# A two-block transformer kernel: two thirds of the modulation vectors move from matrix products to row sums on the vector engine, and neighbouring transposes are issued in common runs

## The chip, the cores and the metric

One core of a Trainium2 chip runs the whole program. Its engines work side by side, each in the order of its own instruction list: TensorE (PE, with its weight loads PEld), VectorE (DVE), ScalarE (ACT), GpSimd (POOL), and SyncE (SP), whose queue issues the DMAs. The metric is the device time in microseconds (us); less is better.

## What is computed

Two blocks, each of two layers, over 256 tokens of width 1024. The first block has three kinds of attention, a gate and a layer norm. In the second block 256 context tokens join, and every layer begins with a modulation that depends only on two vectors, `c` and `c_ctx`:

```python
shift_x, scale_x, gate_x = jnp.split(jax.nn.silu(c) @ w_mod + b_mod, 3, axis=-1)
shift_c, scale_c, gate_c = jnp.split(jax.nn.silu(c_ctx) @ w_mod + b_mod, 3, axis=-1)
hx = rms_norm(xs, norm_g) * (1 + scale_x[:, None]) + shift_x[:, None]
hc = rms_norm(cs, norm_g) * (1 + scale_c) + shift_c
px = split_cols(hx @ w_in + b_in)
pc = split_cols(hc @ w_in + b_in)
# px, pc feed a convolution branch, a gated linear attention and an attention
xs = xs + gate_x[:, None] * merge(px, ya_x, yb_x, yc_x)
if need_ctx:                       # layer 0 only
    cs = cs + gate_c * merge(pc, ya_c, yb_c, yc_c)
```

`merge` is `(sigmoid(p13)*ya + sigmoid(p14)*yb + sigmoid(p15)*yc) @ w_out`. `w_mod` is 1024 x 3072 in each layer, so the modulation of both layers reads 24 MB of weights, and each weight takes part in just two products.

## The kernel before, in words

**Large products.** A large product is done as three passes of a reduced-precision format (`mm3`, lines 184 to 186): high times high, high times low, low times high. Each weight unit of 512 KB is loaded by SP into one of RAW = 4 buffers (`wr_...`), cast by ACT into `wh_...` (line 154, WB = 5 buffers) and subtracted by DVE into `wl_...` (line 155, 5 buffers). `WStream` holds one table of all units in the order of use. `get(key)` calls `ahead`, which issues loads up to `ad` table entries and splits up to `asp` entries beyond the one in use: 3 and 2 at first, 6 and 3 from the first block's output product on.

**The modulation.** Each layer has three vectors (s = 0 shift, 1 scale, 2 gate), and each of them is eight units of 512 KB: 48 units in all. `mod_stream` (lines 762 to 788) takes a unit as loaded, without a split, and multiplies it by a narrow stationary operand with `c` and `c_ctx` (line 770, four products of 256 columns, which the trace shows as eight instructions). After eight units ACT copies the sums (line 775), four small products turn them (line 778, tile `modt`), and DVE adds the bias (line 782). The table `FILL` says ahead of which weight unit how many modulation units are worked: all 24 of layer 0 in the second layer of block one, the 24 of layer 1 in block two, 16 in its layer 0 and 8 in its layer 1. `get` of that unit issues them. One PSUM buffer of the five tagged `gm` holds the running sums.

**Block two, layer 0** (`block2`), in its program order: keys (`AKV`, tokens in pairs of 128-token blocks) and queries (`AQ`, `BQ`), convolution inputs (`Va`, `Vb`), attention interleaved with `GK`, `GQ`, `GV` and `ag`; then the merges: branch `m3`/`oa`, gates `gg`, branch `m2`/`og`, `conv_finish`, gates `cg`, branch `m1`/`oc`, and the residual products `o` and `p`. A branch takes two gate units and one output unit in turn, so between `m3_1` and `oc3` there are 43 units. The convolution is 31 taps for each of four blocks, one DVE instruction each (line 1012); 10 are issued with each attention step, 24 with the `gg` gates and 32 among the merges of `m2`; `conv_finish` (from line 1330) needs them all. Layer 1 has the same parts in another order.

**Transposes.** A transpose is a PE instruction that copies a 128-wide tile through PSUM. `post_k` (line 925 on) makes two for each token block, `lrt` (line 938) right after the product and `akt` (line 952) after a norm and a rotation on DVE. In the attention, `weigh` ends with two (`ot`, line 1091) and `scores` with one (`mt`, line 1053).

**Order.** Within each engine the order is fixed when the program is built, by a planner that takes among ready instructions the one that comes first in the program. On the chip each engine then runs its list in that order, and an instruction that has to wait holds all behind it.

Of the kernel before, what the change touches and what calls it, by code (L numbers as in the profile page):

```python
# [33 lines left out]
WLX = 0  # L34
# [5 lines left out]
MORDER = (1, 0, 2)  # L40

FILL = '1B2 2 1E2 3 1D2 3 1F0 2 1G0 2 1H2 1 0Va0 2 0Va1 2 0Va2 2 0GV0 1 0ag0 2 0ag2 2 1GV0 3 1ag0 2 1ag2 2 1A0 1 0BQ2 2 1F2 2 1GK0 1 1B0 1 1A3 5 1C2 1 0ag1 1 1H0 1 0GK0 2'
# [68 lines left out]
class WStream:  # L111
# [46 lines left out]
    def whole(self, key):  # L158

        i = self.idx[key]  # L160
        self.ahead(i)
# [12 lines left out]
    def get(self, key):  # L174
# [4 lines left out]
        self.ahead(i)  # L179
        return self.spl[i]  # L180
# [49 lines left out]
def block1(g, l, xTh, xTl, xtok, W, last, pre_out=lambda: None, hold=None, each=None):  # L230
# [268 lines left out]
    def fox_gates():  # L499
# [24 lines left out]
        nc.tensor.matmul(ps[:, 128:256], lf[:, 0, :], g.ones, start=False, stop=True)  # L524
# [208 lines left out]
def units_mod():  # L733
    return [(f'mod{s}{k}', k, 1, [(D * s, D)]) for s in MORDER for k in range(8)]

# [26 lines left out]
def mod_stream(g, l, W):  # L762

    nc, sp, pp = g.nc, g.sp, g.pp
    for s in MORDER:
# [18 lines left out]
        if s == 1:  # L784

            nc.vector.scalar_tensor_tensor(g.modA[l], g.mod[l][:, ks, :], 1.0,
                                           g.ng[l][:, :, None].to_broadcast([128, 8, 2]), op0=OP.add, op1=OP.mult)
# [3 lines left out]
def norm_prep(g, l, seqs, hT, a, n):  # L791
# [6 lines left out]
    for j, (sT, w) in enumerate(seqs):  # L798
        pr = g.t2([128, 2, 256], f'{nm}pr{j}')
        for i in range(8 // nk):  # L800
# [36 lines left out]
def block2(g, l, hT, res_of, W, out=None, then=lambda x: None):  # L837
# [23 lines left out]
    def tm(key, nch, tbs, n, post, seq=False):  # L861
# [12 lines left out]
        for j in range(h):  # L874
            for tb in tbs:
                part(tb, [j])
        for tb in tbs:
            part(tb, range(h, nch))
            post(ps[tb][:, :n], tb)
# [28 lines left out]
    def rope2(x, nh, tb, which, nm):  # L908
# [10 lines left out]
        nc.vector.tensor_add(x, x, t)  # L919

    def gain(x, nh, which):
        x3 = x.rearrange("p (h d) -> p h d", d=64)
        nc.vector.tensor_mul(x3, x3, g.qkg[l][:, which, None, :].to_broadcast([128, nh, 64]))
# [4 lines left out]
    def post_k(ps, tb):  # L928
# [8 lines left out]
        pt = pp.tile([96, 128], F32, name=f'lrt{l}{tb}', tag='at', bufs=g.AT)  # L937
        nc.tensor.transpose(pt, kl[:, 128:224], idf)
        lr = lrT[:, 128 * tb:128 * tb + 128]
        nc.scalar.copy(lr[0:96], pt)  # L940
        nc.vector.tensor_sub(lr[32:64], pt[32:64], lr[32:64].bitcast(F32))
# [5 lines left out]
        if tb < 2:  # L947
            gain(kb, 2, 1)
        else:
            rope2(kb, 2, tb - 2, 1, f'k{tb}')  # L950
        pt = pp.tile([128, 128], F32, name=f'akt{l}{tb}', tag='at', bufs=g.AT)
        nc.tensor.transpose(pt, kb, idf)
        ts = slice(128 * tb, 128 * tb + 128)
# [4 lines left out]
        nc.vector.tensor_sub(k12[64:128, 0, 1, ts], pt[64:128], k12[64:128, 0, 1, ts].bitcast(F32))  # L958

# [62 lines left out]
    def scores(tb, kv):  # L1022
# [28 lines left out]
        nc.vector.scalar_tensor_tensor(ms[:, 1], mx, -1.0, ms[:, 0].bitcast(F32), op0=OP.mult, op1=OP.subtract)  # L1051
# [4 lines left out]
        yield  # L1056

    def weigh(tb, kv, q1, q2):
# [30 lines left out]
        pt = pp.tile([128, 2, 128], F32, name=nm + 'ot', tag='at', bufs=g.AT)  # L1089
        for i in range(2):  # L1090
            nc.tensor.transpose(pt[:, i, :], o[:, 128 * i:128 * i + 128], idf)
        c = 128 * tb - T0
        nc.scalar.activation(aoT[:, 2 * kv:2 * kv + 2, c:c + 128], pt, AF.Copy, scale=0.5)
        yield

    prev = iter(())
    for tb, kv in [(tb, kv) for tb in TB for kv in range(2)]:
        nxt = scores(tb, kv)
        qs = next(nxt)
        for st in range(4):  # L1100
            next(prev, None)
            next(nxt, None)
        prev = weigh(tb, kv, *qs)
    for _ in prev:
        pass

# [724 lines left out]
```

## Time and profile before

| what | us |
|---|---|
| median of 3 runs | 1193.03 |
| lowest and highest of them | 1192.88, 1195.18 |
| the profiled execution's own time | 1192.62 |
| its span, first to last instruction | 1190.8 |
| PE, DVE, ACT busy | 1168.5, 921.1, 569.5 |

A busy time is the time in which an engine has at least one instruction under way. PE's matmuls overlap, so the cost of one is read from start to start, not from its duration. A stretch is a piece of the span, counted in us from its start.

### The profile page before, as it was taken

The page shows a single profiled execution, that of the slowest core. Times are in us where ns is not written, and L with a number is a line of the kernel's source. Part 1 is how long each engine was busy: PE and PEld are TensorE (multiplying, and loading weights), DVE is VectorE, ACT ScalarE, POOL GpSimd, SP SyncE. Part 2 cuts the span into 40 slices and gives each one's busy share as a digit, 9 for nine tenths or more (in the row PEclk, how much of TensorE's full clock was granted, in tenths as well). Part 3 has the DMA queues.
Part 4 walks back from the last instruction along what each step waited for, and adds up shares of the span by engine and source line. Part 5 has one row for each costly group of instructions (what it writes and reads, how often), then busy time and mean ns, then how long its engine had stood idle before and what let it go on. Part 6 is the DMA issues. An engine that isn't in the chain of part 4 may idle for free.

```text
span 1190.8 us, 20632 instructions
## 1 busy us (share of the span) xinstructions
PE 1168.5 (98%) x8024; PEld 975.7 (82%) x8024; DVE 921.1 (77%) x2051; ACT 569.5 (48%) x1024; POOL 11.2 (1%) x42
## 2 busy tenths in 40 slices
PE   8999999999999999999999999999999999999998
PEld 6788777677887777767887888888999778999998
DVE  6996766967799859989545986755799897896984
ACT  5556634456555433247444422433455534855552
POOL 0000000000000000000000000000000000000000
PEclk9999999999999999999999999999999999999999
DMA  7634566465555642024221232325545333554552
GB/s 263 224 125 127 186 207 225 155 229 195 177 194 181 230 137 89 19 73 145 68 84 59 89 100 78 106 89 177 178 142 186 96 107 123 179 162 127 174 176 72
DMA packets 47538, 171.33 MB, mean 144 GB/s; under 512 B 5260, under 2 KB 5900, under 8 KB 46672
## 3 DMA queue, kind: packets, MB, share of 16 engines
q1 hardware_dynamic: 47440, 170.01, 43.7%
q8 instruction: 63, 1.03, 0.3%
q14 instruction: 35, 0.29, 0.1%
HBM read 167.89 MB, written 2.10 MB: 143 GB/s over the span
## 4 chain that ended last, share of the span: by engine, by line
PE 76%; DVE 11%; DMA 6%; ACT 5%; issue 2%; SPq 0%; ACTq 0%; DVEq 0%
PE f0m L186 3%; PE f0m L185 3%; PE f0m L184 3%; PE f1m L186 2%; PE f1m L184 2%; PE f1m L185 2%; PE po L185 1%; PE po L186 1%; PE po L184 1%; PE mod L770 1%; PE go L186 1%; PE go L185 1%; PE go L184 1%; PE yog L186 1%; PE yoc L186 1%
## 5 line engine op out<-in xcount | busy, mean ns | idle before, releaser
L1012 DVE SCALAR_TENSOR_TENSOR ucv<-up,par,ucv 128x512 f32<-128x512 f32 (+1 forms) x240 | 147.3, 614 | 2.8
L184 PE MATMUL f0m<-hTh,wh_0m 128*128 128x512 f32 x192 | 75.1, 391 | 0.0
L185 PE MATMUL f0m<-hTl,wh_0m 128*128 128x512 f32 x192 | 75.1, 391 | 0.0
L186 PE MATMUL f0m<-hTh,wl_0m 128*128 128x512 f32 x192 | 74.8, 390 | 0.0
L184 PE MATMUL f1m<-hTh,wh_1m 128*128 128x256 f32 x192 | 54.9, 286 | 0.1
L186 PE MATMUL f1m<-hTh,wl_1m 128*128 128x256 f32 x192 | 54.8, 286 | 0.0
L185 PE MATMUL f1m<-hTl,wh_1m 128*128 128x256 f32 x192 | 54.5, 284 | 0.0
L154 ACT CAST wh_0m<-wr_0m 128x1024 fp32r<-128x1024 f32 x24 | 25.1, 1047 | 55.9 <-PE f0m L185 14.5
L155 DVE TENSOR_TENSOR wl_0m<-wr_0m,wh_0m 128x1024 fp32r<-128x1024 f32 x24 | 29.3, 1222 | 18.2 <-ACT wh_0m L154 18.1
L184 PEld LDWEIGHTS f0m<-hTh,wh_0m 128*128 128x128 f32 x192 | 36.1, 188 | 7.4
L185 PEld LDWEIGHTS f0m<-hTl,wh_0m 128*128 128x128 f32 x192 | 36.1, 188 | 7.3
L186 PEld LDWEIGHTS f0m<-hTh,wl_0m 128*128 128x128 f32 x192 | 36.1, 188 | 7.3
L184 PEld LDWEIGHTS f1m<-hTh,wh_1m 128*128 128x128 f32 x192 | 36.8, 191 | 0.5 <-ACT wh_1m L154 0.3
L186 PEld LDWEIGHTS f1m<-hTh,wl_1m 128*128 128x128 f32 x192 | 36.7, 191 | 0.2 <-DVE wl_1m L155 0.2
L185 PEld LDWEIGHTS f1m<-hTl,wh_1m 128*128 128x128 f32 x192 | 36.8, 191 | 0.1
L154 ACT CAST wh_1m<-wr_1m 128x1024 fp32r<-128x1024 f32 x24 | 24.9, 1049 | 24.4 <-PE f1m L185 7.6
L155 DVE TENSOR_TENSOR wl_1m<-wr_1m,wh_1m 128x1024 fp32r<-128x1024 f32 x24 | 29.3, 1221 | 8.6 <-ACT wh_1m L154 8.4
L155 DVE TENSOR_TENSOR wl_0o<-wr_0o,wh_0o 128x1024 fp32r<-128x1024 f32 x8 | 9.8, 1224 | 13.2 <-ACT wh_0o L154 13.2
L1413 DVE SCALAR_TENSOR_TENSOR xT<-po,mod,xT 128x256 f32<-128x256 f32 x16 | 7.7, 483 | 14.3 <-PE po L186 14.3
L185 PE MATMUL po<-mgl,wh_0o 128*128 128x256 f32 x64 | 18.2, 285 | 0.0
L186 PE MATMUL pp<-mgh,wl_0p 128*128 128x256 f32 x64 | 18.2, 284 | 0.0
L185 PE MATMUL pp<-mgl,wh_0p 128*128 128x256 f32 x64 | 18.2, 284 | 0.0
(1857 smaller groups left out, 3960.6 us busy)
## 6 DMA issues: line engine op xcount, KB each, us to landing
wr_0mod<-in_wm_dram SPq DMA_DIRECT2D x24, 512.0 KB, 4.5
wr_1mod<-in_wm_dram SPq DMA_DIRECT2D x24, 512.0 KB, 3.7
wr_0m<-in_w_dram SPq DMA_DIRECT2D x24, 512.0 KB, 3.5
wr_1m<-in_w_dram SPq DMA_DIRECT2D x24, 512.0 KB, 3.5
wr_0O<-in_w1o_dram SPq DMA_DIRECT2D x8, 512.0 KB, 3.6
wr_1O<-in_w1o_dram SPq DMA_DIRECT2D x8, 512.0 KB, 3.6
wr_0o<-in_wo_dram SPq DMA_DIRECT2D x8, 512.0 KB, 3.6
wr_0p<-in_wo_dram SPq DMA_DIRECT2D x8, 512.0 KB, 3.7
```

Of the source, the lines that this page charges most:

```text
L154: g.nc.scalar.copy(wh, r)
L155: g.nc.vector.tensor_sub(wl, r, wh.bitcast(F32))
L184: nc.tensor.matmul(out, lh, rh, start=start, stop=False)
L185: nc.tensor.matmul(out, lh, rl, start=False, stop=False)
L186: nc.tensor.matmul(out, ll, rh, start=False, stop=stop)
L770: nc.tensor.matmul(ps[32 * q:32 * q + 32], g.cz[:, k // 2, 2 * (k % 2):2 * (k % 2) + 32], w[:, 0, 256 * q:256 * q + 256], start=k == 0, st ...
L1012: yield nc.vector.scalar_tensor_tensor(o, src, dw[:, i, j:j + 1], o, op0=OP.mult, op1=OP.add)
L1413: nc.vector.scalar_tensor_tensor(r[:, f, :], ps[:, :256], g.mod[l][:, 16 + f, w:w + 1], r[:, f, :], op0=OP.mult, op1=OP.add)
```

## The change

Modulation: only the 16 units of layer 0's scale and shift stay products (`MODP`), in the second layer of block one, at the places where they were. The other 32 units (layer 0's gate, all of layer 1) are laid out with the output index on the partitions (`pack_mod`), 256 outputs by 512 inputs in a unit. `mod_dots` multiplies each with the vector `c` or `c_ctx`, spread over all partitions, and sums the rows: four DVE instructions of 128x512 with a running sum to a unit. The vector is loaded and its silu made twice, once for each half. `DFILL` spreads the 32 units evenly over the 43 units from layer 0's `m3_1` to `oc3`; they are issued by `get` of that unit and stand in the load table one entry later (`LATE`).

Further: modulation entries no longer count in the look-ahead (`behind`); `wl` has four buffers instead of five (`WLX`); the all-ones matrix shrinks to a column, and the rotation table is loaded when needed, once for each layer, instead of lying in the constants.

Transposes: `post_k` returns its last DVE instruction and a `flip`, and both blocks' flips are issued together after the second; the first waits for the second block's DVE work. In the attention the `ot` transposes of one step wait for the `mt` transpose's input of the next. In `norm_prep` and `conv_finish` the first PE instruction of a run waits for the last DVE input of that run.

```diff
-WLX = 0
+WLX = -1
-FILL = '1B2 2 1E2 3 1D2 3 1F0 2 1G0 2 1H2 1 0Va0 2 0Va1 2 0Va2 2 0GV0 1 0ag0 2 0ag2 2 1GV0 3 1ag0 2 1ag2 2 1A0 1 0BQ2 2 1F2 2 1GK0 1 1B0 1 1A3 5 1C2 1 0ag1 1 1H0 1 0GK0 2'
+FILL = '1A0 1 1A3 5 1B0 1 1B2 2 1E2 3 1C2 1 1D2 3'
+DFILL = ((32, '0m3_1', '0oc3'),)
+LATE = 1
+MODP = [(0, 1), (0, 0)]
+MODD = [(*m, c, h) for ms, hs in (([], (0, 1)), ([(0, 2), (1, 1), (1, 0), (1, 2)], (1, 0)))
+        for h in hs for m in ms for c in range(4)]
...
+    def behind(self, i, n):
+        while n and i < len(self.table) - 1:
+            i += 1
+            n -= self.table[i][0] not in self.f32
+        return i
     def ahead(self, i):
-        while self.nd < min(len(self.table), i + self.ad + 1):
+        while self.nd < min(len(self.table), self.behind(i, self.ad) + 1):
             self._dma()
-        while self.ns < min(len(self.table), i + self.asp + 1):
+        while self.ns < min(len(self.table), self.behind(i, self.asp) + 1):
...
         self.ahead(i)
+        for _ in range(self.dots.pop(key, 0)):
+            next(self.dotstream)
         return self.spl[i]
...
+def mod_dots(g, W):
+    nc, sp = g.nc, g.sp
+    junk = g.cp.tile([128, 512], BF, name='modj')
+    have, seen = None, set()
+    for l, s, c, h in MODD:
+        if h != have:
+            cb, have = sp.tile([128, 2, 512], F32, name=f'modc{l}{s}{h}', tag='modc', bufs=1), h
+            nc.sync.dma_start(cb, g.csrc[1024 * h:1024 * h + 1024][None, :].to_broadcast([128, 1024])
+                              .rearrange("p (w k) -> p w k", w=2))
+            for w in range(2):
+                t = g.t2([128, 512], f'modt{l}{s}{h}{w}')
+                nc.scalar.activation(t, cb[:, w], AF.Tanh, scale=0.5)
+                nc.vector.scalar_tensor_tensor(cb[:, w], t, 1.0, cb[:, w], op0=OP.add, op1=OP.mult)
+        x = W.whole(f'{l}mod{s}{c}{h}')
+        m = g.mod[l][:, 8 * s:8 * s + 8, :]
+        second = (l, s, h ^ 1) in seen
+        if c == 0:
+            half = sp.tile([128, 8, 2], F32, name=f'modh{l}{s}', tag='modh', bufs=2) if second else m
+        for b in range(2):
+            for w in range(2):
+                nc.vector.scalar_tensor_tensor(junk, x[:, b], 0.5, cb[:, w], op0=OP.mult, op1=OP.mult,
+                                               accum_out=half[:, 2 * c + b, w:w + 1])
+        if c == 3:
+            seen.add((l, s, h))
+            if second:
+                nc.vector.tensor_add(m, m, half)
+                nc.vector.tensor_add(m, m, g.bmod[l][:, 8 * s:8 * s + 8, None].to_broadcast([128, 8, 2]))
+                if s == 1:
+                    mod_gain(g, l)
+        yield
...
         for tb in tbs:
             part(tb, range(h, nch))
-            post(ps[tb][:, :n], tb)
+            late.append(post(ps[tb][:, :n], tb))
+        if isinstance(late[0], tuple):
+            for i, (_, flip) in enumerate(late):
+                first = flip()
+                if i == 0:
+                    g.wait(first, late[1][0])
...
         for st in range(4):
-            next(prev, None)
-            next(nxt, None)
+            flip = next(prev, None) or flip
+            got = next(nxt, None) or got
+        if flip is not None:
+            flip(got)
...
-CST = [('ident', 128), ('ones', 128), ('rope2', 256), ('gmask', 256), ('sel8', 8), ('hm', 4), ('zc', 2)]
+CST = [('ident', 128), ('ones', 1), ('gmask', 256), ('sel8', 8), ('hm', 4), ('zc', 2)]
...
+    rc = g.t2([128, 2, 2, 64], f'rope2c{l}')
+    nc.sync.dma_start(rc, g.rope2src.rearrange("p (a t d) -> p a t d", a=2, t=2))
```

## Rows read from the trace of the kernel before

**Rows 1.** Page, part 1: busy us (share of the span) and instructions of each engine.

```profile
PE 1168.5 (98%) x8024; PEld 975.7 (82%) x8024; DVE 921.1 (77%) x2051; ACT 569.5 (48%) x1024; POOL 11.2 (1%) x42
```

**Rows 2.** Busy times by stretch: length, each engine's busy us (instructions), clock, DMA share, GB/s.

```profile
240.00:300.00 60.00, 55.36 (x449) 43.28 (x451) 40.19 (x93) 37.23 (x104) 0.17 (x2) 1.00 0.59 200
340.00:400.00 60.00, 59.08 (x348) 47.23 (x347) 58.08 (x218) 35.17 (x65) 0.00 (x0) 1.00 0.56 190
440.00:560.00 120.00, 119.19 (x900) 90.71 (x899) 109.05 (x181) 52.95 (x86) 3.23 (x7) 1.00 0.24 77
560.00:655.00 95.00, 93.55 (x730) 76.66 (x728) 51.95 (x106) 42.39 (x87) 0.00 (x0) 1.00 0.24 73
655.00:737.00 82.00, 81.76 (x366) 67.74 (x367) 65.19 (x88) 27.45 (x37) 0.17 (x2) 1.00 0.31 97
737.00:773.00 36.00, 35.91 (x173) 29.47 (x172) 30.21 (x76) 14.04 (x19) 0.46 (x6) 1.00 0.30 88
773.00:827.00 54.00, 54.00 (x240) 44.73 (x239) 25.27 (x30) 18.77 (x24) 0.00 (x0) 1.00 0.40 134
900.00:1000.00 100.00, 99.05 (x807) 81.44 (x807) 91.69 (x239) 41.75 (x76) 1.15 (x3) 1.00 0.35 114
```

**Rows 3.** PE's modulation products alone, by stretch: length, busy us (instructions), clock, DMA.

```profile
248.00:345.00 97.00, 5.10 (x64) 1.00 0.57 193
345.00:420.00 75.00, 4.28 (x64) 1.00 0.58 200
420.00:560.00 140.00, 5.92 (x64) 1.00 0.28 91
560.00:900.00 340.00, 0.00 (x0) 1.00 0.34 107
900.00:1010.00 110.00, 4.89 (x64) 1.00 0.39 125
```

**Rows 4.** PE's `modt` products alone, by stretch, in the same columns.

```profile
200.00:345.00 145.00, 1.22 (x8) 1.00 0.56 191
345.00:560.00 215.00, 1.08 (x8) 1.00 0.39 129
560.00:1010.00 450.00, 0.62 (x4) 1.00 0.35 111
```

**Rows 5.** PE in order of time around one `lrt` transpose: start, us, instruction.

```profile
365.17 0.29 PE L184 MATMUL t0AKV<-wh_0AKV,hTh 128*128 128x288 f32 x1
365.30 0.30 PE L185 MATMUL t0AKV<-wl_0AKV,hTh 128*128 128x288 f32 x1
365.71 0.29 PE L938 MATMUL lrt<-cst,kb 128*96 128x128 f32 x1
365.75 0.38 PE L186 MATMUL t0AKV<-wh_0AKV,hTl 128*128 128x288 f32 x1
365.97 0.30 PE L184 MATMUL t0AKV<-wh_0AKV,hTh 128*128 128x288 f32 x1
```

**Rows 6.** PE in order of time around the two `ot` transposes of a step.

```profile
448.34 0.39 PE L186 MATMUL f0GK<-hTh,wl_0GK 128*128 128x512 f32 x1
448.57 0.40 PE L184 MATMUL f0GK<-hTh,wh_0GK 128*128 128x512 f32 x1
448.80 0.38 PE L1091 MATMUL at000ot<-cst,at000o 128*128 128x128 f32 x2
448.94 0.36 PE L1044 MATMUL at001s<-k,at001q 128*128 128x256 f32 x1
449.14 0.28 PE L1045 MATMUL at001s<-k,at001q 128*128 128x256 f32 x1
```

**Rows 7.** DVE instructions by line: count, ns least/median/most, first and last start, shape.

```profile
L669 DVE SCALAR_TENSOR_TENSOR mx<-xtok,go x4: 680/681/689, 150.4 to 162.8; 128x512 f32<-128x512 f32 x4
L669 DVE DVE_READ_ACCUMULATOR mx<-xtok,go x4: 81/84/84, 151.0 to 163.4; 128x1 f32 x4
L431 DVE SCALAR_TENSOR_TENSOR lscr<-par x4: 206/216/218, 79.5 to 238.5; 128x64 f32<-128x64 f32 x4
L1274 DVE SCALAR_TENSOR_TENSOR qgg<-gtgg,qgg x4: 681/688/690, 656.8 to 673.2; 128x512 f32<-128x512 f32 x4
L1274 DVE SCALAR_TENSOR_TENSOR qgc<-gtgg,qgc x4: 418/419/420, 1065.0 to 1073.6; 128x256 f32<-128x256 f32 x4
```

**Rows 8.** The end of the convolution chain on DVE, and its first user on PE.

```profile
767.31 1.35 DVE L220 SCALAR_TENSOR_TENSOR ycg<-gtcg,ycg 128x512 fp32r<-128x512 f32 x2
...
773.30 0.39 PE L184 MATMUL yoc<-ycg,wh_0oc 128*128 128x512 f32 x1
```

**Rows 9.** Waits of the load queue, whole span: engine, line, releaser: us, times, longest.

```profile
SPq L130 <- DVE wl_0m L155: 134.7, 22, 13.1
SPq L130 <- PE mod L770: 90.4, 25, 14.2
```

**Rows 10.** The 31-tap convolution on DVE within 548 to 800 us.

```profile
L1012 DVE SCALAR_TENSOR_TENSOR ucv<-up,par,ucv 128x512 f32<-128x512 f32 x47 | 35.2, 749 | 0.6
```

More of the change, by code (lines that the diff above doesn't have):

```diff
@@ L733, in units_mod, with pack_mod @@
 def units_mod():
-    return [(f'mod{s}{k}', k, 1, [(D * s, D)]) for s in MORDER for k in range(8)]
+    return [(f'mod{s}{k}', k, 1, [(D * s, D)]) for _, s in MODP for k in range(8)]
+def pack_mod(l, w):
+    wt = w.T.reshape(24, 128, 2, 512)
+    parts = [pack(w, units_mod())] if l == 0 else []
+    for ll, s, c, h in MODD:
+        if ll == l:
+            f = 8 * s + 2 * c
+            parts.append(wt[f:f + 2, :, h].transpose(1, 0, 2).reshape(-1))
+    return np.concatenate(parts)
 def _seq(n, k):
@@ L946, in post_k, with flip_k @@
         nc.vector.tensor_mul(k3, k3, ky[:, :, None].to_broadcast([128, 2, 64]))
[L947 to L950, printed above, removed]
+        done = gain(kb, 2, 1) if tb < 2 else rope2(kb, 2, tb - 2, 1, f'k{tb}')
+        return done, lambda: flip_k(kl, tb)
+    def flip_k(kl, tb):
+        kb = kl[:, 0:128]
+        pl = pp.tile([96, 128], F32, name=f'lrt{l}{tb}', tag='at', bufs=g.AT)
+        first = nc.tensor.transpose(pl, kl[:, 128:224], idf)
         pt = pp.tile([128, 128], F32, name=f'akt{l}{tb}', tag='at', bufs=g.AT)
         nc.tensor.transpose(pt, kb, idf)
+        lr = lrT[:, 128 * tb:128 * tb + 128]
+        nc.scalar.copy(lr[0:96], pl)
+        nc.vector.tensor_sub(lr[32:64], pl[32:64], lr[32:64].bitcast(F32))
         ts = slice(128 * tb, 128 * tb + 128)
@@ L1088, in weigh, with flip @@
         nc.vector.tensor_mul(o.rearrange("p (h d) -> p h d", d=64), po[:, :, 0:64], rc.to_broadcast([128, 4, 64]))
[L1089 to L1094, printed above, removed]
+        def flip(after):
+            pt = pp.tile([128, 2, 128], F32, name=nm + 'ot', tag='at', bufs=g.AT)
+            for i in range(2):
+                t = nc.tensor.transpose(pt[:, i, :], o[:, 128 * i:128 * i + 128], idf)
+                if i == 0 and after is not None:
+                    g.wait(t, after)
+            c = 128 * tb - T0
+            nc.scalar.activation(aoT[:, 2 * kv:2 * kv + 2, c:c + 128], pt, AF.Copy, scale=0.5)
+        yield flip
     prev = iter(())
@@ L1348, in conv_finish @@
             for tb in range(NT // 128):
-                nc.tensor.transpose(pt[:, 128 * tb:128 * tb + 128], ns[tb][:, 128 * f:128 * f + 128], idf)
+                t = nc.tensor.transpose(pt[:, 128 * tb:128 * tb + 128], ns[tb][:, 128 * f:128 * f + 128], idf)
+                if f == tb == 0:
+                    g.wait(t, normed)
             tz = t2(f'cvz{f}', NT)
@@ L1654, in setup2 @@
     g.rowsrc = {}
+    g.rope2src = ins['rope2']
     rp = ins['rowp']
@@ L1726, in program @@
     nc = g.nc
-    mods = sum((table(ins[f'wm_{l}'], f'{l}', units_mod()) for l in range(2)), [])
-    f32 = {e[0] for e in mods}
+    mods = table(ins['wm_0'], '0', units_mod())
+    dots, at = [], [len(mods) * 128 * 1024, 0]
+    for l, s, c, h in MODD:
+        dots.append((f'{l}mod{s}{c}{h}', ins[f'wm_{l}'], at[l], 2, 512))
+        at[l] += 128 * 1024
+    f32 = {e[0] for e in mods + dots}
     fs = FILL.split()
@@ L1746, in program @@
         seq += o
+    keys = [e[0] for e in seq]
+    use, at, m = {}, {}, 0
+    for n, a, b in DFILL:
+        a, b = keys.index(a), keys.index(b) + 1
+        for i in range(n):
+            k = a + i * (b - a) // n
+            at.setdefault(keys[k + LATE], []).append(dots[m])
+            use[keys[k]] = use.get(keys[k], 0) + 1
+            m += 1
+    assert m == len(dots)
     tab, m = [], 0
@@ L1749, in program @@
         n = fills.get(e[0], 0)
-        tab += mods[m:m + n] + [e]
+        tab += mods[m:m + n] + at.get(e[0], []) + [e]
         m += n
@@ L1755, in program @@
     W = WStream(g, tab, looks, f32, fills)
-    W.stream = itertools.chain(mod_stream(g, 0, W), mod_stream(g, 1, W))
+    W.stream, W.dots, W.dotstream = mod_mm(g, W), use, mod_dots(g, W)
     xsp = g.dram.tile([128, 2048], F32, name='xsp')
```

64 lines of the change are left out of this document (35 added, 29 removed).

## The prediction

> **What bounds the kernel now.** I read the page's first part, then the busy times by stretch, then PE's own order in time where the change cuts in. PE is busy 98% of the span, DVE 77%, ACT 48% [rows 1]. The stretches say the same nearly everywhere: PE has 119.2 of 120 us in the attention of block two's layer 0 and 81.8 of 82 among the merges of `m2` [rows 2]. So whatever is taken out of PE's list shortens the kernel, as long as the other engines keep up. The reader should see in the same rows that DVE is close behind in places: 58.1 of 60 us at 340 to 400, 109.1 of 120 at 440 to 560, 91.7 of 100 at 900 to 1000, but only 52.0 of 95 at 560 to 655 and 25.3 of 54 at 773 to 827. The clock column is 1.00 in all of them, so the clock plays no part. The question is an exchange: PE time saved at one price, DVE time paid at another, in a stretch where DVE may or may not have it to give.
>
> The sum is made against the profiled execution, 1192.6 us (span 1190.8 and 1.8 around it); the median of the runs is 0.4 above it, which I add at the end. About 0.2%, 2.4 us, is what a measurement of this kernel can tell from no change.
>
> **PE: 32 units of products leave.** Their busy time by stretch is 5.1 us (8 units) at 248 to 345, 4.3 and 5.9 us (8 each) at 345 to 420 and 420 to 560, and 4.9 us (8) at 900 to 1010 [rows 3]: 20.2 us, 0.63 to a unit. Four of the six `modt` groups leave too, about 0.6 us each: one of the two at 200 to 345, both at 345 to 560, one later, 2.3 us [rows 4]. Gross 22.5 us. What arrives differs by stretch.
> - 248 to 345: gross 5.7. PE is already idle 4.6 of 60 us here, and DVE and ACT have a third free [rows 2]. The queue of loads waits 90 us in the whole span for modulation products to give their buffers back [rows 9], so eight units less also bring weights earlier. Against that, products that filled the waits of the attention saved nothing. I take 4, between 0 and 7.
> - 345 to 420: gross 4.8. DVE is full for most of it, with 1.9 us idle in 60 [rows 2], so PE would mostly wait instead. I take 1.5, between 0 and 4.8.
> - 420 to 560: gross 6.4. DVE's 109 us still fit into 113.6. I take 5.5, between 2 and 6.4.
> - 900 to 1010: gross 5.5. DVE's 91.7 us of 100 fit into 95. I take 4.5, between 1 and 5.5.
>
> Together 15.5 us, between 3 and 23.7.
>
> **PE: transposes in common runs.** The `lrt` transpose starts 0.41 us after a product that is otherwise followed in 0.13, and the second product behind it starts 0.67 after the first where 0.26 would do: one transpose alone costs 0.41 us [rows 5]. Of a pair behind each other (`ot`) the same reckoning gives 0.57 us from 448.57 to 449.14, against 0.23 and 0.12 for two such products, 0.22 for two: 0.11 each [rows 6]. The keys have 16 transposes. At 0.41 each they are 6.6 us, in four runs of four (0.41 and three times 0.11) 3.0, at most 3.6 less. Half lie in the stretch where DVE is full, and some are paired already, so I take 1.5, between 0 and 3.6. The twelve `ot` pairs are at 0.11 already and have nothing to give. Their later start, and that of the keys, adds waits on PE for DVE; queued behind them is the next weight product, so a wait that the planner has placed too early stops the whole stream. The rows show 0.3 us for one such wait [rows 5]; I count 0, between 1 lost and 1 gained, the waits in `norm_prep` and `conv_finish` included.
>
> **Small parts.** The rotation table comes by its own load before the keys, behind weight loads on SP; the constants get smaller by 196 KB at the start; `wl` loses a buffer, so a split may wait for the unit four before it, with three units of PE time (16 us) still ahead of its use. No row prices these. The nearest are the waits of the load queue for a buffer, 4 to 6 us each in the mean and 14 at most, which PE, busy 98%, hardly felt [rows 1, 9]. I take 0, between 1 gained and 2 lost.
>
> **DVE: 32 units of row sums come in.** A unit is four instructions of 128x512 with a running sum. The nearest row is 681 ns, and the read of the sum behind it is another 84 ns: 0.765 us [rows 7]. 128 of them are 98 us. Two loads of the vector add four instructions at 0.69, some 3 us. They are spread from `m3_1`, which starts near 560 us, to `oc3`, near 822: 0.74 of a unit, 2.3 us, to each of 43 weight units of 5.4 us.
> - 560 to 655: 52.0 us there, and 12 weight units bring 27: 79 of 95. It fits, and as at least one of the four load buffers must go on carrying weights, row sums can run at most some three units ahead.
> - 655 to 737: 65.2 there, of which most of the 35 us of taps [rows 10]; 15 weight units bring 34. That is 99 in 82, 17 too many. Three units done ahead take off 9. 8 us stay, and the last taps end that much later.
> - 737 to 773: the convolution's chain has 30.2 of 36 us. It ends at 768.7 (two instructions from 767.31, 1.35 us) and PE wants it at 773.3 [rows 8]: 4.6 us to spare. Six weight units bring 4.5 units, 13.7 us; in the program they stand behind the chain, but they fill its gaps, and each can hold it for up to 0.77. With some seven such gaps, 5 us.
> - 773 to 827: 25.3 there, ten weight units bring 7.4 units, 22.6, and most of the 13.7 left over: 61 in 54, the rest slides into the residual products.
>
> So the chain is late by 8 + 5 - 4.6, about 8.5 us, and PE waits for it; I take 9 with the two vector loads in it. The lower bound is 0, if the row sums find the free time at 560 to 655; below that I see nothing, since no work leaves this stretch. The upper is 17 + 13.7 - 4.6 = 26, if none runs ahead and all go before the chain.
>
> **Sum.** 1192.6 - 15.5 - 1.5 + 9 = 1184.6, against the median 1185.0.
>
> [...] The rows show a 512-wide instruction with two SBUF sources at 688 ns and a 256-wide one at 419, so 1.05 ns to a column; at 64 columns this gives 217, and the one row with two fp32 SBUF sources and a running sum has 216 [rows 7]. [...]
>
> **Rivals.**
> 1. *The free time is found.* The planner sees the same gaps as I do, and the row sums go where DVE idles. For it: 43 us free at 560 to 655, 29 at 773 to 827. Against: the buffers. Then the cost is 0 and the gains come near gross: 22.5 + 1.5 off, 1169.
> 2. *DVE becomes the bound among the merges, and the kernel is slower.* The row sums go before the chain, the taps before `conv_finish` and the splits behind them come late, and PE stands. It is dearer than what is saved from 17 us of delay on; at the upper bound of 26 the time is 1192.6 - 17 + 26, about 1202. For it: 99 us of work in 82, and a load buffer is held until its sums are done, which stops weights as well. Against: sums that belong to later units are lower in order than the chain.
> 3. *Nothing comes through.* PE waits for DVE in 340 to 560 and 900 to 1000 for as long as it saves, say 8 us net, and the merges take the 8 back: 1192 to 1194. For it: DVE at 91 to 97% there. It holds also if the units taken out had been filling waits.
> [...]
>
> **How the numbers follow.** Forecast (1176 to 1190): 0.45. Rival 1 (1165 to 1176): 0.24. Rival 2 (1195.5 to 1210): 0.17. Rival 3 (1190.6 to 1195.4): 0.11. Rival 4: 0.03. Faster by over 0.2% is the forecast and rival 1, less a little of the forecast's upper end: 0.67. Within 0.2%: rival 3 and that end, 0.12. Slower: 0.21. The range for 8 in 10 leaves out rival 4, the far part of rival 2 and the lower part of rival 1: 1166 to 1203.
>
> **What would show it.** In the changed profile PE's busy time falls by some 20 us and DVE's rises by about 100, to near 1020. [...] The time from `m3_1` to `oc3` was 262 us: if it stays there, rival 1; near 271, the forecast; 280 and more, rival 2, with PE waiting on DVE for taps or `wl` splits. The stretch from the start of block two to `m3_1` should be shorter by some 7 us and that of layer 1's attention by 4 to 5; if they are not, rival 3. The `lrt` and `akt` rows should show four in a run. I am wrong altogether if PE's idle time grows where nothing was changed, above all in the first 240 us.

## The result and the profile after

| | before | after |
|---|---|---|
| median, us | 1192.95 (1191.39 to 1195.18) | 1174.28 (1172.98 to 1184.17) |
| profiled execution, us | 1192.62 | 1174.49 |
| its span, us | 1190.8 | 1172.7 |

The ratio is 0.9866, with a 95% interval of 0.9823 to 0.9909: about 18 us less. Measured once more beside other kernels, the changed kernel took 1175.69 (ratio 0.9845, 0.9820 to 0.9870). Single times of one and the same kernel scatter by some us (the 1184.17 had a granted clock of 0.994, the other three 0.998 to 1.000), so I read stretches within the profiles and not single times.

The first part of the page after answers to [rows 1]:

```profile
PE 1147.7 (98%) x7752; PEld 969.1 (83%) x7752; DVE 995.4 (85%) x2315; ACT 570.5 (49%) x1024; POOL 11.2 (1%) x42
```

PE has 20.8 us less to do and is as busy as before, 98%. DVE has 74 us more. The line numbers have moved: `mm3` is 198 to 200 now, the `wl` split 159, the row sums are 842, `lrt` and `akt` 1020 and 1022, the taps 1086.

The same profile cut by stages follows; each begins with the first product of that stage on PE: block one (from its second group of weights on, `g0B`), the keys and the attention of block two's layer 0, its merges, then residual and attention of layer 1, and the merges of layer 1 (to 0.1 us before the end). Columns as in [rows 2].

```profile
19.00:335.80 316.80, 308.69 (x1921) 243.62 (x1921) 249.59 (x618) 172.47 (x374) 3.34 (x14) 1.00 0.53 175
335.80:535.50 199.70, 196.75 (x1268) 158.62 (x1268) 177.86 (x431) 94.18 (x157) 3.24 (x7) 1.00 0.30 97
535.50:812.50 277.00, 273.59 (x1540) 225.44 (x1539) 256.74 (x576) 111.09 (x177) 0.62 (x8) 1.00 0.48 153
812.50:995.40 182.90, 179.70 (x1404) 161.78 (x1403) 162.86 (x405) 91.90 (x150) 3.15 (x7) 1.00 0.40 127
995.40:1172.60 177.20, 172.62 (x1567) 168.78 (x1566) 137.78 (x273) 90.21 (x154) 0.00 (x0) 1.00 0.45 146
```

Before, the same five stages took 322.5, 211.4, 273.9, 185.6 and 177.5 us. The differences are -5.7, -11.7, +3.1, -2.7 and -0.2; with 0.9 us before the first of them they make the 18.1 by which the span shrank. 20 us came off where products left, and the stretch that received 94 us of vector work gave back three.

Lengths of the stages in all profiles, in us, from the start of each stage's first product (a table of my own, to 0.1 us or so; one profile of each kernel, which is not always the execution nearest the median: that of `half_again` took 1209.12, of `late0` 1181.19, of `old_look` 1179.40 and of `runs_only` 1186.40):

| kernel | block one | keys, attention 0 | merges 0 | attention 1 | merges 1 | median |
|---|---|---|---|---|---|---|
| before | 322.5 | 211.4 | 273.9 | 185.6 | 177.5 | 1192.95 |
| after | 316.8 | 199.7 | 277.0 | 182.9 | 177.3 | 1174.28 |
| after_again | 313.4 | 201.0 | 277.7 | 182.8 | 177.4 | 1175.69 |
| none32 | 316.7 | 199.9 | 273.4 | 182.9 | 177.2 | 1171.05 |
| quarter | 314.7 | 200.8 | 281.2 | 183.0 | 176.8 | 1177.78 |
| half_again | 317.1 | 200.4 | 303.9 | 186.5 | 177.5 | 1204.35 |
| spread | 314.2 | 204.1 | 274.0 | 182.6 | 177.8 | 1175.34 |
| late0 | 320.7 | 200.9 | 278.5 | 182.7 | 177.2 | 1174.83 |
| old_look | 318.4 | 199.7 | 277.3 | 182.8 | 177.4 | 1177.29 |
| no_runs | 314.7 | 199.8 | 277.1 | 185.0 | 176.4 | 1174.04 |
| runs_only | 320.7 | 210.6 | 271.6 | 187.6 | 177.6 | 1190.15 |
| taps16 | 314.0 | 200.9 | 277.2 | 185.7 | 174.0 | 1173.98 |
| all48 | 334.6 | 199.6 | 276.7 | 182.7 | 177.1 | 1193.31 |
| eight_later | 315.5 | 201.0 | 274.8 | 181.0 | 210.2 | 1204.57 |

In block one the kernels whose text is the same there differ by up to 7 us (313.4 to 320.7), so a difference of 2 in that column says nothing. In the other columns equal texts agree within 1.5, except where sums left over from the merges run on into the next stage (`half_again`, attention 1).

### The profile page after: what moved, and what is told of

It is laid out like the page before. It is cut to its first block, busy times and chain, and to the rows that moved or that the text cites. A ratio compares the mean times of both kernels' runs of the same rounds, so it can differ in the third digit from the quotient of the medians.

```text
span 1172.7 us, 20383 instructions
## 1 busy us (share of the span) xinstructions
PE 1147.7 (98%) x7752; PEld 969.1 (83%) x7752; DVE 995.4 (85%) x2315; ACT 570.5 (49%) x1024; POOL 11.2 (1%) x42
## 4 chain that ended last, share of the span: by engine, by line
PE 71%; DVE 16%; ACT 5%; DMA 5%; issue 2%; SPq 0%; ACTq 0%; DVEq 0%
PE f0m L198 2%; PE f0m L200 2%; PE f0m L199 2%; DVE modj L842 2%; PE f1m L200 1%; PE f1m L199 1%; PE f1m L198 1%; DVE ucv L1086 1%; PE po L198 1%; PE po L200 1%; PE po L199 1%; PE go L199 1%; PE go L198 1%; PE go L200 1%; DMA wr_1mod<-in_wm_dram 1%
## 5 line engine op out<-in xcount | busy, mean ns | idle before, releaser
L842 DVE SCALAR_TENSOR_TENSOR modj<-wr_1mod,modc 128x512 bf16<-128x512 f32 x96 | 66.1, 688 | 8.3 <-DMA wr_1mod<-in_wm_dram 7.2
L158 ACT CAST wh_0m<-wr_0m 128x1024 fp32r<-128x1024 f32 x24 | 25.1, 1048 | 41.1 <-DMA wr_0m<-in_w_dram 28.2
L1382 ACT ACTIVATE mtm<-f0m,hbin 128x512 f32<-128x512 f32 x24 | 16.5, 686 | 22.8 <-PE f0m L200 20.5
L842 DVE SCALAR_TENSOR_TENSOR modj<-wr_0mod,modc 128x512 bf16<-128x512 f32 x32 | 22.0, 688 | 0.5
```

The lines of the kernel that those rows point to most:

```text
L158: g.nc.scalar.copy(wh, r)
L842: nc.vector.scalar_tensor_tensor(junk, x[:, b], 0.5, cb[:, w], op0=OP.mult, op1=OP.mult, accum_out=half[:, 2 * c + b, w:w + 1])
L1382: nc.scalar.activation(sg, pm, AF.Tanh, scale=0.5, bias=hb[:, blk(n, f)])
```

## The experiments

**What do the row sums cost?** In `none32` the 32 units are neither loaded nor summed; the modulation is filled with a constant.

```diff
-DFILL = ((32, '0m3_1', '0oc3'),)
+DFILL = ()
...
+    for l in L:
+        nc.vector.memset(g.mod[l], 0.5)
+    nc.vector.memset(g.modA[1], 0.5)
```

> The changed kernel without the 32 row-sum units: neither loads nor sums, so layer 0's gate and layer 1's modulation are constants. Theory A (the products' leaving gave its full 22.5 us and the row sums cost only the 3.1 us by which the stretch from the first m3 unit to the first residual product is longer, 277.0 against 273.9): 1171, that stretch back at 274. Theory B (the row sums cost about the 9 us that I had taken, and another part of the change, the common runs or the look-ahead, gave the rest): 1165 or less.

Measured: 1171.05 us (1169.84 to 1174.45), ratio 0.9822 (0.9793 to 0.9852). The merges take 273.4 us, as before the change. So 94 us of vector work, together with their loads, cost 3.6 us in their stage. The medians differ by 3.2, or 4.6 against the second measurement of the changed kernel; their intervals overlap, and it is the stage that shows the cost (276.7 to 277.7 in the profiles with the same merges). A kernel that takes them for nothing would gain some 3 to 4 us and no more.

**Less of the same work.** `quarter` keeps all loads and does one of the four sums of a unit; copies stand for the rest.

```diff
-        for b in range(2):
-            for w in range(2):
-                nc.vector.scalar_tensor_tensor(junk, x[:, b], 0.5, cb[:, w], ..., accum_out=half[:, 2 * c + b, w:w + 1])
+        nc.vector.scalar_tensor_tensor(junk, x[:, 0], 0.5, cb[:, 0], ..., accum_out=half[:, 2 * c, 0:1])
+        nc.vector.tensor_copy(half[:, 2 * c + 1, :], ...)
+        nc.vector.tensor_copy(half[:, 2 * c, 1:2], ...)
```

> The changed kernel with all loads of the 32 units but one row sum of four in each; the other three results are copies of the first, so the modulation is wrong. VectorE loses 74 us of work, the load queue none. Theory A, if the cost of the row sums is VectorE's time: 1171, as without the units. If it is the loads (VectorE waited 7.2 us for four of them): 1173 to 1175, and the run without units is faster than this one.

Measured: 1177.78 us (1174.09 to 1185.94), ratio 0.9883 (0.9847 to 0.9918). The merges are not shorter but 4 us longer, 281.2, though DVE is busy only 203 of them. First DVE's waits of this run, then its order around one of them, then three windows there (columns as in [rows 2]):

```profile
DVE modj L840 <- DMA wr_1mod<-in_wm_dram: 31.2, 14, 3.7
```

```profile
723.23 0.69 DVE L840 SCALAR_TENSOR_TENSOR modj<-wr_1mod,modc 128x512 bf16<-128x512 f32 x1 [3.19 <-DMA wr_1mod<-in_wm_dram]
...
724.70 0.69 DVE L1422 BATCH_NORM_STATS2 cvs<-cvt 128x6 f32<-128x512 f32 x1
...
729.59 0.63 PE L1420 MATMUL cvt<-cst,ucv 128*128 128x128 f32 x4 [3.34 <-DVE cv01t L215]
```

```profile
725.50:729.50 4.00, 0.74 (x4) 0.28 (x2) 4.00 (x27) 0.00 (x0) 0.00 (x0) 1.00 0.27 107
729.50:733.00 3.50, 3.41 (x12) 2.79 (x13) 3.50 (x12) 1.17 (x2) 0.00 (x0) 0.60 0.31 60
733.00:740.00 7.00, 7.00 (x34) 5.77 (x33) 5.77 (x20) 2.10 (x3) 0.00 (x0) 0.95 0.62 198
```

A unit's load takes some 4 us to land (the median is 4.4 us for layer 0's units and 3.7 for layer 1's), and its sums now 0.77 instead of 2.9. DVE waits 31 us for loads, 14 times, where the changed kernel waits 7.2 us, 4 times. One of these waits, 3.19 us, stands ahead of the statistics of the convolution. They come late, PE stands 3.34 us for them, and behind that its clock is granted 0.60 for 3.5 us. That one stop is most of the 4 us: PE's idle time in the stage is 6.3 us instead of 3.4, and it is busy 1.3 longer. A short instruction that waits is dearer here than a long one that runs. (The times alone don't show it: the intervals of the two ratios overlap.)

**More of the same work.** `half_again` does two of the four sums of each unit twice, 64 instructions, about 49 us at the price of the prediction.

```diff
+            nc.vector.scalar_tensor_tensor(junk, x[:, b], 0.5, cb[:, 1], op0=OP.mult, op1=OP.mult,
+                                           accum_out=half[:, 2 * c + b, 1:2])
```

> The changed kernel with two of every four row sums done twice: 64 more of 0.77 us, 49 us more for VectorE, which has 20 us free of 277 in that stretch. If VectorE is the bound there, as the rival of the prediction had it, the rest stops TensorE: 25 to 35 us more, 1200 to 1209. If sums that belong to later units simply slide behind (into the residual products, 10 us free): below 1190.

Measured: 1204.35 us (1202.22 to 1209.12), ratio 1.0101 (1.0071 to 1.0130): 30 us more than the changed kernel and slower than before. DVE had 277.0 - 256.7 = 20.3 us free in the merges after the change. 64 more at 0.73 us from start to start are 47, which leaves 27 too many, and the stage grew by 27, the next by 3.6, in a profile that is the slowest of the six executions. That the two 27 agree is in part chance: PE stands 15 us longer in the stage (18.5 against 3.4), and for the same products it is busy 12 us longer (285.4 against 273.6), at a mean clock of 0.98. PE's longest waits are now for weights, and its clock falls where it stands:

```profile
PE f0m L198 <- ACT wh_0m L158: 3.7, 3, 2.1
PE yog L198 <- ACT wh_0og L158: 3.6, 1, 3.6
PE f0m L200 <- DVE wl_0m L159: 3.3, 6, 0.9
```

```profile
720.00:760.00 40.00, 32.44 (x125) 24.60 (x123) 37.02 (x121) 7.09 (x8) 0.17 (x2) 0.87 0.43 132
```

This is rival 2: the splits of the weights come late, and PE stands. Its waits for them are 14.2 us in this stage, where the changed kernel lists none. ACT's casts wait longer for their loads too (42.1 us for `wh_0m` against 28.2). But the load queue's waits for buffers that sums hold did not grow (47.9 us against 73.5), so the second reason of rival 2, the held buffers, isn't shown. The changed kernel stands some 20 us of vector work in front of all this.

**Where the sums stand.** `spread` puts six of the units into the stage of layer 0's keys and attention and thins the `gg` and `m2` part; `late0` puts the sums' loads one table entry earlier; `eight_later` leaves 24 units in layer 0's merges and does the eight of layer 1's gate among layer 1's merges.

```diff
-DFILL = ((32, '0m3_1', '0oc3'),)
+DFILL = ((6, '0Va2', '0GQ1'), (10, '0m3_1', '0oa3'), (4, '0gg0', '0og3'), (12, '0cg0', '0oc3'))   # spread
```

> The changed kernel with the 32 units laid out otherwise: 6 from the second convolution input to the last query unit (VectorE 25 of 40 us busy there), 10 in branch m3, 4 from the gg gates to og3, where the taps are, 12 from the cg gates on. If VectorE's time among the merges costs the 3 us, 1171 to 1172; if it is the loads or the planner's order, no gain: 1173 to 1176.

```diff
-LATE = 1
+LATE = 0
```

> The changed kernel with each row-sum unit one entry earlier in the load table. VectorE waited 7.2 us for four such loads in the changed kernel and 31.2 for fourteen in the run with a quarter of the sums, which was no faster for its 74 us less of work. If the loads' lateness is the cost, these waits fall and the time goes to 1172 or 1173; if the units only hold the four load buffers longer, weights come late instead: 1175 to 1178.

```diff
-DFILL = ((32, '0m3_1', '0oc3'),)
+DFILL = ((24, '0m3_1', '0oc3'), (8, '1m3_1', '1og3'))
-... ([(0, 2), (1, 1), (1, 0), (1, 2)], (1, 0)))
+... ([(0, 2), (1, 1), (1, 0)], (1, 0)), ([(1, 2)], (0, 1)))
```

> 24 units of row sums among layer 0's merges as in the changed kernel; the eight units of layer 1's gate, which nothing needs before layer 1's residual, among layer 1's merges, from m3 to og. There VectorE was busy 137.8 of 177.3 us in the changed kernel and TensorE stood for 4.7. Theory A, the 3 us that the row sums cost are paid where VectorE is full (conv_finish and its neighbourhood) and are less with 24 units there: layer 0's merges 274 to 275.5 instead of 277.0, layer 1's merges unchanged at 177.3, whole 1171 to 1173. Rival, the cost is per unit wherever it stands, as with the units spread into the attention: layer 1's merges 1 us longer or more, whole 1174 to 1176.

Measured: `spread` 1175.34 us (1173.27 to 1183.85), ratio 0.9867 (0.9840 to 0.9894). The merges are down to 274.0 and DVE waits for no load of a sum, but the keys and the attention take 204.1 instead of 199.7: the cost moved and did not go. `late0` 1174.83 us (1173.13 to 1181.19), ratio 0.9849 (0.9828 to 0.9869), with DVE's waits for loads where they were, 7.0 us in 4: no change.

`eight_later` took 1204.57 us (1200.60 to 1209.66), ratio 1.0096 (1.0068 to 1.0125). Half of theory A held: with 24 units layer 0's merges take 274.8. But layer 1's merges take 210.2 instead of 177.3, which neither theory had. PE's two longest waits from 990 us on, the stretch in which it stood most, and two instructions of ACT:

```profile
PE gn11t L1346 <- DVE gw L1343: 7.3, 1, 7.3
PE gl100cum L1237 <- DVE la L1230: 5.5, 1, 5.5
```

```profile
1100.00:1115.00 15.00, 8.37 (x79) 7.19 (x77) 2.31 (x13) 4.20 (x18) 0.00 (x0) 0.61 0.00 1
```

```profile
1042.72 1.15 ACT L833 ACTIVATE modt<-modc 128x512 f32<-128x512 f32 x2 [2.50 <-DMA modc<-in_ccr_dram]
1043.78 1.06 ACT L1224 ACTIVATE me<-z 128x512 f32<-128x512 f32 x2
```

What PE waits for is the chain of the gated linear attention (`gl`, `gn`), which goes from engine to engine in short steps. The first `gg` product starts 34.6 us after layer 1's first merge product instead of 45.7: PE had been given its products ahead of that chain. So when the chain ran, little was left to run beside it. DVE is busy 2.3 of 15 us there; it is not its load that costs. The trace shows where the chain was held. Its first product on PE, `z`, is done at 979 us, but `me`, the step of ACT that takes it up, comes at 1043.78, where the changed kernel needs 1.2 us (981.73 to 982.88). The trace lists no wait of its own for it; it stands in ACT's list right behind `modt`, the silu of a third load of the vector. The changed kernel loads the vector twice, this layout three times; the load goes into the one buffer `modc` and was issued at 1035.5, when the sums before it were done. So this run doesn't price eight units of sums among layer 1's merges: it shows what it costs when a chain stands in a list behind a late load. Why the planner put `me` there stays open, and no run tries this layout without the third load.

**All 48 units.** `all48` turns the last 16 units into sums too, in block one's attention.

```diff
-FILL = '1A0 1 1A3 5 1B0 1 1B2 2 1E2 3 1C2 1 1D2 3'
-DFILL = ((32, '0m3_1', '0oc3'),)
+FILL = ''
+DFILL = ((16, '1A0', '1G1'), (32, '0m3_1', '0oc3'))
...
-MODP = [(0, 1), (0, 0)]
-MODD = [(*m, c, h) for ms, hs in (([], (0, 1)), ...
+MODP = []
+MODD = [(*m, c, h) for ms, hs in (([(0, 1), (0, 0)], (0, 1)), ...
```

> All 48 units as row sums on VectorE, the first 16 too, in block one's attention. TensorE loses about 16 products of 0.68 us, 10.8 us, at 165 to 300; VectorE gets 16 times 4 times 0.77 us, 49 us, in some 130 us where it was busy about two thirds. Theory A, that what VectorE gets in free time costs next to nothing as in the 32 units: 1164 to 1168. Rival, that the weights' loads and the vector engine's queue in front of the attention hold it up as in the run with a quarter of the sums: 1174 to 1190.

Measured: 1193.31 us (1190.73 to 1196.29), ratio 1.0005 (0.9987 to 1.0022), 19 us above the changed kernel, nearly all of it in block one (334.6 against 316.8). PE's waits at 160 to 300 us, and three windows:

```profile
PE da10s L420 <- DVE fvn L359: 4.7, 1, 4.7
PE g1D L199 <- DVE wl_1D L159: 4.6, 3, 3.9
PE g1A L198 <- ACT wh_1A L158: 3.0, 1, 3.0
```

```profile
165.00:185.00 20.00, 14.92 (x56) 12.00 (x57) 18.88 (x48) 6.85 (x11) 0.00 (x0) 0.83 0.46 135
...
215.00:240.00 25.00, 20.30 (x87) 14.91 (x86) 23.96 (x93) 10.29 (x21) 0.00 (x0) 0.86 0.50 166
240.00:265.00 25.00, 17.96 (x92) 12.53 (x91) 23.68 (x71) 7.45 (x11) 0.35 (x4) 0.93 0.48 150
```

Here the rival held in kind; the time is 3 us above its range. DVE is at 94 to 96% in these windows, where it had been at 73 to 80% (in the changed kernel 31.9 of 40 us at 200 to 240, 43.6 of 60 at 240 to 300); PE waits for short steps of the attention and for splits, and its clock is granted 0.83 to 0.93 there. The 10.8 us taken from PE are gone and 18 more. Whether DVE's queue or the loads did it the run doesn't separate.

**The common runs.** `no_runs` puts the transposes of the changed kernel back as they were; `runs_only` is the kernel before with the common runs alone.

```diff
-            late.append(post(ps[tb][:, :n], tb))
-        if isinstance(late[0], tuple): ...
+            post(ps[tb][:, :n], tb)
...
-            flip(got)
...
```

> The changed kernel with the transposes issued as before (keys, attention outputs, norm and convolution). By the prediction the runs give 1.5 us, 0 to 3.6, all of it at the keys: 1176 (1174 to 1178). Theory B: they give what the stretch from the keys to the first m3 unit gained beyond the products' price, and that stretch is 4 us or more longer. Rival: their waits cost as much as they save, 1172 to 1174.

> The kernel before with the common runs of transposes alone (keys, attention outputs, norm, convolution). The prediction took 1.5 us for them, 0 to 3.6: 1190 to 1191. The run with the runs undone in the changed kernel left it where it was, so the rival: 1192 to 1193, within 0.2% of the kernel before.

Measured: `no_runs` 1174.04 us (1172.24 to 1176.88), ratio 0.9842 (0.9815 to 0.9869): as the changed kernel. `runs_only` 1190.15 us (1186.40 to 1194.27), ratio 0.9979 (0.9963 to 0.9995): 2.5 us less than the runs of before beside it by the ratio, between 0.6 and 4.4; the medians differ by 1.7. By its profile the keys and the attention gave 0.8, the merges 2.3 (271.6 against 273.9), and layer 1's attention lost 2.0: over block two, the only place with common runs, 847.4 against 848.4 us. The rest of that profile's 6 us lies ahead of block two, where nothing was changed. On top of the modulation nothing of the runs can be seen.

**The look-ahead.** `old_look` counts modulation units in the look-ahead again.

```diff
-            n -= self.table[i][0] not in self.f32
+            n -= 1
```

> The changed kernel with the modulation units counted again in the look-ahead of loads and splits. They stand only in block one's second layer and among the merges now. If block one's gain of 6.6 us (5.7 by the products' price) came from earlier loads, 1176 to 1178 with the start of block two 2 to 3 us later; if from the products alone, that start stays at 336 and only the merges can change, by a weight that comes later: 1174 to 1177.

Measured: 1177.29 us (1172.64 to 1179.99), ratio 0.9870 (0.9847 to 0.9893), every stage as after, as far as block one's scatter of 7 us lets one say so: the 2 or 3 us that the first theory asked for there could hide in it. It does nothing that can be seen.

**Layer 1's attention.** `taps16` does 16 instead of 19 taps at a step of it.

```diff
-TAPS = (10, 19)
+TAPS = (10, 16)
```

> The changed kernel with 16 instead of 19 convolution taps on the vector engine at each step of layer 1's attention; what is left over follows later. In the changed kernel the stretch from the residual's first product to layer 1's merges is 182.9 us, 2.7 shorter than before where 5.5 us of transposes left it. Theory A, VectorE binds there (busy 56.8 of 60 us at 940 to 1000, TensorE 59.5): fewer taps let TensorE through, the stretch becomes 180 to 181 and the whole 1171 to 1173. Theory B, the wait there is one of order (a joint pair of transposes waits for the later of two tiles) and not of VectorE's load: the stretch stays at 182 to 184, the whole at 1174 to 1176; if the taps moved into the merges then bind there, up to 1180.

Measured: 1173.98 us (1173.23 to 1176.28), ratio 0.9854 (0.9837 to 0.9870). The attention stage grew to 185.7 and the merges behind it fell to 174.0, as some products changed places; the two together are 359.7 against 360.2. Theory A falls: less vector work there gives nothing.

> The changed kernel once more, beside the one with eight units later and on the same chip. Both theories: 1172 to 1176.

Measured: 1175.69 us (1172.92 to 1176.10), beside `eight_later`. Of the kernels that compute the whole, none beats it by more than the scatter.

## Why the prediction was right, and where it was not

The direction, the exchange and the range held: PE is the bound, its products left, the sums found room. The time came 11 us lower than 1185, outside the forecast's own window (1176 to 1190, given 0.45) and in that of rival 1 (1165 to 1176, given 0.24): the gains came near gross and the cost was small, though not 0. From the start of `m3_1` to that of `oc3` it took 262.1 us before and 265.0 after, where rival 1 had asked for 262 and the forecast for 271. PE's idle time in the first 240 us, the sign of being wrong altogether, is 9.0 against 7.9 us, and 7.2 in `none32`, whose text is the same there: scatter. Point by point:

**DVE's term, 9 taken, 3.1 measured.** This is the largest miss. The step that failed is "8 us stay, and the last taps end that much later", in the stretch where I had found 99 us of work in 82. DVE's time on the sums alone in the changed kernel, by windows of 20 us (length, busy, clock, DMA):

```profile
560.00:580.00 20.00, 12.53 (x36) 1.00 0.58 161
580.00:600.00 20.00, 9.37 (x29) 1.00 0.65 208
...
640.00:660.00 20.00, 0.00 (x0) 1.00 0.43 131
660.00:680.00 20.00, 4.17 (x12) 1.00 0.31 94
680.00:700.00 20.00, 3.46 (x10) 1.00 0.45 144
700.00:720.00 20.00, 9.74 (x28) 1.00 0.48 159
...
760.00:780.00 20.00, 11.14 (x32) 1.00 0.58 181
```

Evenly spread it would be some 6.4 in each (89 us in 277). The sums stand thick at 560 to 600 and after 760, and thin at 640 to 700, where most of the taps are. The first row below is the stretch that I had reckoned with (7 us after the first `gg` product to the first `cg` product, 655 to 737 before), the other two its end and what follows:

```profile
633.00:721.70 88.70, 88.37 (x401) 73.14 (x400) 83.14 (x159) 31.65 (x54) 0.17 (x2) 1.00 0.41 131
...
666.00:722.00 56.00, 56.00 (x255) 46.51 (x255) 55.02 (x107) 14.27 (x17) 0.17 (x2) 1.00 0.43 141
722.00:758.00 36.00, 34.97 (x164) 28.60 (x163) 35.93 (x102) 13.51 (x17) 0.46 (x6) 1.00 0.39 132
```

The 99 us in 82 became 83 in 88.7. Only 20.7 us of them are sums, where I had put 34, and 25 after the running ahead. 13 of the 32 units were done before this stretch, four more than an even spread puts there (I had allowed three); and inside it sums slipped up to 9 us behind the weight unit ahead of which the program has them, which my working did not allow: it put them before the taps. The stretch is also longer than before, with PE busy in all but 0.3 us of it: 88.4 us of products where there had been 81.8. That the sums go where DVE has time is what rival 1 said. In the last 56 us of the stretch DVE is full and PE loses nothing, and from 722 to 758 it loses 1.0 us, at the convolution's end where I had reckoned 8.5. PE's longest waits in the whole stage are short ones for DVE:

```profile
PE gl010cum L1237 <- DVE la L1230: 1.1, 1, 1.1
PE cvt L1420 <- DVE cv01y L225: 1.0, 1, 1.0
```

Over the stage PE's idle time is 3.4 us against 1.8 before, and it is busy 273.6 against 272.1; these two make the 3.1. Why it is busy 1.5 us more with the same products stays open.

**The price of a sum, right and a little high.** DVE in order of time, two ordinary instructions of that width and then two sums:

```profile
562.39 0.68 DVE L1395 SCALAR_TENSOR_TENSOR acc<-mtm,yoa 128x512 f32<-128x512 f32 x1
562.99 0.69 DVE L1313 TENSOR_TENSOR gl00am<-gl00am,gl00am 128x512 f32<-128x512 f32 x1
...
564.72 0.69 DVE L842 SCALAR_TENSOR_TENSOR modj<-wr_0mod,modc 128x512 bf16<-128x512 f32 x1
565.33 0.08 DVE L842 DVE_READ_ACCUMULATOR modj<-wr_0mod,modc 128x1 f32 x1
565.45 0.69 DVE L842 SCALAR_TENSOR_TENSOR modj<-wr_0mod,modc 128x512 bf16<-128x512 f32 x1
```

I added the durations to 0.765; from start to start it is 0.73 (564.72 to 565.45), since they overlap, 94 us for 128. The overlap is one reason why DVE's busy time rose by 74 us (79 against `none32`) and not by 100. An ordinary one takes 0.60 from start to start (562.39 to 562.99), so summing costs 0.13 more. Its 0.69 us is the duration without a sum too [rows 7]. No row or run shows the term that rival 4 (given 0.03) was worked out from; what the runs showed in its place is this 0.13 us.

**Products at 345 to 560, 1.5 + 5.5 taken, 11.7 measured.** The step that failed is "DVE is full for most of it, with 1.9 us idle in 60 [rows 2], so PE would mostly wait instead". I read that from 340 to 400. The same trace of before, cut from the keys to the first linear attention product and from there to the merges, and then the last 35 us of the first piece alone, says otherwise:

```profile
342.40:435.20 92.80, 91.03 (x514) 72.42 (x512) 74.34 (x254) 47.64 (x81) 0.00 (x0) 1.00 0.56 191
435.20:553.80 118.60, 117.67 (x895) 89.18 (x892) 107.98 (x180) 47.94 (x79) 3.23 (x7) 1.00 0.26 85
...
400.00:435.20 35.20, 34.35 (x179) 27.20 (x177) 18.45 (x42) 14.18 (x19) 0.00 (x0) 1.00 0.58 194
```

and of after, same cut:

```profile
335.80:423.30 87.50, 84.66 (x430) 70.34 (x429) 71.93 (x254) 45.97 (x79) 0.00 (x0) 1.00 0.47 153
423.30:535.50 112.20, 112.09 (x842) 88.28 (x840) 105.93 (x178) 48.21 (x79) 3.24 (x7) 1.00 0.17 53
```

DVE was busy 74.3 of 92.8 us: 18 free, and 16.8 of them behind the 60 us that I had looked at. PE's busy time fell by 6.4 and 5.6 and the pieces by 5.3 and 6.4: all of the gross, 11.2, came through. `no_runs` and `old_look` leave this stage at 199.8 and 199.7, so neither the common runs nor the look-ahead made it. That the free time behind the full 60 us let the products' time through is my reading: in the first piece PE's idle time did rise, from 1.8 to 2.8 us, but by no more than that. A stretch that is full for 60 us isn't full between two points at which PE must have something.

**Products at 248 to 345, 4 taken, 5.7 measured** in one profile each, 6.6 against the mean of the profiles with this text (315.9 from nine): near the gross of 5.7, but with a scatter of block one as large as itself beside it.

**Layer 1, 4.5 taken, 2.7 measured.** PE's busy time fell by 4.9, but its idle time rose from 1.0 to 3.2. The waits in that stage after; before, the only one listed was 0.8 us for `akt`:

```profile
PE lrt L1020 <- DVE kb L995: 1.0, 1, 1.0
PE f1Vb L198 <- ACT up L1073: 0.6, 1, 0.6
```

The 1.0 is the first transpose of a common run, which waits for the later of two blocks, and the next weight product stands behind it: the mechanism I had counted at 0. Without the common runs (`no_runs`) other waits come in its place (1.3 and 0.9 us). Over both stages of layer 1 the four kernels take 363.1 us (before), 365.2 (common runs alone), 361.4 (products gone, no common runs) and 360.2 (both). So with the common runs the products' leaving gives 5.0 of the gross 5.5, and without them 1.7; the runs cost 2.1 before the change and give 1.2 after it. The two parts don't add, and which of them lost the missing 2 us stays open: products that had filled waits, as the prediction had it for rival 3, would do it, and so would the runs' own waits. DVE's load isn't the cause (`taps16`), though DVE had 25 us free in this stage before (160.5 busy of 185.6).

**Transposes, 1.5 taken, 0 to 2.5 measured:** 2.5 by the ratio of `runs_only`, nothing by `no_runs`. The size can't be told better, and the place isn't the keys, where I had it. The run there isn't one of four: three transposes stand at 0.11 to 0.12 from each other, in all four runs, and the fourth comes 0.8 to 1.6 us later.

```profile
369.81 0.39 PE L200 MATMUL t0BQ<-wh_0BQ,hTl 128*128 128x512 f32 x1
370.09 0.29 PE L1020 MATMUL lrt<-cst,kb 128*96 128x128 f32 x1
370.21 0.27 PE L1022 MATMUL akt<-cst,kb 128*128 128x128 f32 x1
370.32 0.27 PE L1020 MATMUL lrt<-cst,kb 128*96 128x128 f32 x1
...
370.67 0.40 PE L199 MATMUL t0BQ<-wl_0BQ,hTh 128*128 128x512 f32 x1
```

From 369.81 to 370.67 two products are issued, which otherwise take 0.46 us: the three transposes cost 0.40 together, where my reckoning gives 0.63 and where the single one of [rows 5] cost 0.41. But before the change the 16 weren't all alone: five of them stood 0.11 to 0.17 us behind another, and 16 transposes are now four runs of three and four single ones.

**Small parts, 0 taken.** The look-ahead gives nothing. The lost `wl` buffer can be felt on DVE, whose splits now wait for PE to be done with an older unit (4.3 us for `wl_0GK`, 4.3 and 3.3 for `wl_0GQ`; before, no such wait was listed), but not on PE, whose waits for splits are 0.7 and 0.5 us against 0.5 and 0.2. Neither it nor the rotation table was tried alone.

Rival 3 is out as a whole: nothing was eaten up in the attention of layer 0, and about half in layer 1. Rival 2 didn't decide here, and `half_again` shows that its mechanism works once it has some 20 us too many to place.

## What to carry to other kernels

Work taken from the bounding engine came through in full in layer 0, although the other engine was full for 60 us there, because it had free time elsewhere between two points at which the first must have its results; so measure that time between those points, not over a round window inside them. Free time alone is no promise: in layer 1's attention it was there too, and only half of the saving came through. Work put on the other engine cost 3 us in 94 up to its free time; 47 us more, 27 beyond it, cost 30. Here it had to stand beside long products, and off the queues that a chain of short steps needs: in block one's attention 16 units cost 19 us net, and where layer 1's linear attention stood behind a late load of the vector, its stage took 33 us more. What an engine waited for counted more than how long it worked: in `quarter` DVE waited 3.19 us for one load, what stood behind it in DVE's list came late, and PE stood 3.34 us.

## What the runs showed of the hardware that was not expected

In four runs stops of PE cost more than their length. After the 3.34 us in `quarter` the granted clock was 0.60 over the next 3.5 us; in `eight_later` it was 0.61 over the 15 us in which PE was busy 8.4, in `all48` 0.83 over 20 us with 14.9 busy, and in `half_again` 0.87 over 40 us with 32.4 busy. There, behind waits of 1.35 and 0.53 us, products of 512 columns followed each other at 0.43 us (744.86 to 745.29) instead of 0.23 (740.50 to 740.73). In [rows 2] and in the changed kernel's stages, where PE is seldom idle, the clock is 1.00. And the running sum over two fp32 sources was cheap, 0.13 us on 512 columns (0.73 from start to start against 0.60).
